# Final norm's squares summed feature-major, masks and scratch tiles prepared earlier, residual stores on ScalarE's queue

## The chip, the cores and the metric

The kernel runs on one core of a Trainium2 chip. A core has a matrix engine (TensorE, PE in the profile, with its weight loads PEld), three engines that work on 128-partition tiles (VectorE or DVE, ScalarE or ACT, GpSimd or POOL) and a fifth that only issues transfers (SyncE or SP). Every engine runs its own instruction list in order; engines wait for one another by semaphores. Transfers are put on queues by SP, ACT or POOL and moved by 16 DMA engines. The metric is device time in microseconds of one execution; less is better. Each time below is the median of several runs, or that of one profiled execution where it says so.

## What is computed

One inference step of a two-layer decoder in float32: 8 x 8 sample tokens, 16 meta tokens and a prompt of 1024, with a width of 1024.

```
def run_trunk(h, C0, n0, m0, lead, attend, prm):
    ...
            a, (C, n, m) = mlstm_mixer(rmsnorm(h, prm['norm_a'][i]), C0[i], n0[i], m0[i], lead, ...)
            h = h + a
    ...
            h = h + fox_mixer(rmsnorm(h, prm['norm_b'][j]), shared, attend,
                              prm['w_qo_b'][j], prm['q_norm_b'][j], prm['w_out_b'][j])
        h = h + swiglu(rmsnorm(h, prm['norm_ffn'][l]), prm['w_gate_up'][l], prm['w_down'][l])
        if l == N_A_LAYERS - 1:
            shared = shared_kv(h, prm['norm_kv'], prm['w_kvf'], prm['b_fg_b'], prm['k_norm_b'])
    y = rmsnorm(h, prm['norm_final'])
```

Layer A (`mlstm_mixer`) is a recurrence over chunks with 8 heads, whose gates go through a soft cap and a log-sigmoid; it returns the states C, n and m. `rmsnorm` divides by the root of the mean square over the 1024 features and multiplies by a gain. Layer B (`fox_mixer`) is attention with a per-row log-forget value over shared keys and values; the samples also attend to paged caches. `swiglu` has an inner width of 2816.

## The kernel before

Tokens are held as nine tiles (`TT`): tile 0 has the 64 sample and 16 meta tokens, tiles 1 to 8 have 128 prompt tokens each. For the FFN, the 1104 tokens are cut into four slices of 276 (`TS`). The residual H is feature-major, 8 blocks of 128 features by tokens, in SBUF as `vA` in the first layer and `Ht` in the second, and it is parked in DRAM as `hD`. A product is made of three matmuls over split operands (`mm3`, L192 to L194: high by high, low by high, high by low); a split is one ACT copy to the rounded format (L254, L266) and one DVE subtraction (L255, L267). The FFN saves products by sums of quarter blocks of the operands: `PairWeights` makes the weights' sums, `TwoNorms` those of two normed slices (`T0A`, `T0B` in the first layer, `T1A`, `T1B` in the second), the products arrive in PSUM as `m` (L1397) and `dps` (L1730).

In order of time:

- `load_x` turns the input to feature-major (`hps`, `xps`) and stores it to `hD` (L662). `phase_a` projects the values for four column groups c = 3, 0, 1, 2; with c = 3 come the gates.
- A second loop projects the query and key tiles; at its twelfth step `row_mask` (L2146 to L2151) builds two masks: POOL fills and selects, DVE reduces. The log-sigmoid of the gates (L276 to L285, result `lf_tm`) and the transposes and scans that follow (`rps` L902, scans L910 to L914, `eA`, `stk`) run beside it.
- The recurrence takes nine chunks. `chunk_scores` makes decayed scores `eb`; `f(n)` puts n steps of the output gates' projection (`mmA`) into TensorE's list as filler, out of a fixed stock, and the rest follows at the end. ACT squares the outputs for the head norm with a sum (L1256, scratch tag `jk`); the final n state goes through `nnP` and `noP`, which use the same tag. `norm_heads` and the gated heads (`ghps`, `ogeb`, `ogqk`) follow.
- The output projection adds to H (`pops`), with its weights (`wo`) split on the way in layer B; four loads of H from `hD` stand among the weight loads on SP's queue.
- In the FFN's last part (54 rounds, `seq`) each round multiplies one loaded part, `hr` from DRAM, split by ACT and DVE, with one weight part; the last rounds add to H. In the first layer `beside` puts pieces of the next norm between matmuls: root, diag (L370), spread (L377, a matmul that spreads one row over partitions into `nps`). Squares for it are summed by `add_sq` (L335 to L346). Finished slices go to `hD` (L1745, four stores on POOL's queue, on which the `hr` loads stand, too).
- `first_values` and three further groups project the shared values; after the first, c = 3, `forget` turns the log-forget values to heads on partitions (`fgps` L2082), scans them (L2087, `cnB`) and turns part of it back (`fgcq`).
- Sample attention masks queries by copying them into a zeroed tile `qmt` (L2346 memset, L2350 copies), one tile per group of four heads. Cached keys are turned by `ktp` (L2227) and copied out by `kT` (L2228). Prompt attention follows.
- `final` makes the last norm: it turns H back to tokens on partitions (`fin` L1793), squares on ACT with a sum (L1812), root, reciprocal, scales on DVE (L1818) and stores (L1823). For the tokens of tiles 6, 7 and 8 this comes after the last round.

The engines other than TensorE, and all queues, are ordered by a scheduler from estimated costs; TensorE's own order is written out by hand in the parts named here.

Of the kernel before, what the change touches and what calls it, by code (L numbers as in the profile page):

```python
# [17 lines left out]
P = 128  # L18
# [75 lines left out]
class TwoNorms:  # L94
# [30 lines left out]
    def first(self):  # L125
        self.sub(self.y1[:, self.lo], self.y2[:, self.lo], self.y1[:, self.lo])
        self.net.nc.scalar.copy(self.T[1][0], self.y1[:, self.lo])
# [12 lines left out]

    def second_c(self):
        self.low(self.x[1][:, self.lo], self.y2[:, self.lo], self.x[0][:, self.lo])
# [33 lines left out]
class Net:  # L176
# [292 lines left out]
    def mlp(self, H, raws, w, l, heads=None, cb=None):  # L469
# [5 lines left out]
        with self.pool(self.uid("nsp")) as sp, self.pool(self.uid("npp"), bufs=2, space=PSUM) as pn:  # L475
# [14 lines left out]
            with ExitStack() as c:  # L490
# [13 lines left out]
                if heads:  # L504
                    for m in range(KT):
                        for z in range(2):
                            nc.sync.dma_start(ws[m][z].bitcast(F32), self.woD[m][:, z])
                else:
                    rp = raws_open.enter_context(self.pool(self.uid("woraw"), side="right"))
                    rs = [rp.tile([P, KT, P], F32, name=self.uid("woraw")) for _ in range(6)]  # L510
                    rs = [cut(slots[0]), cut(slots[1]), *(rs[x] for x in (3, 4, 5, 2, 1, 0))]
                    for m in range(KT):
                        nc.sync.dma_start(rs[m], w[:, m * P : (m + 1) * P].rearrange("(k p) n -> p k n", p=P))
                        self.split(rs[m], *ws[m])
                        if m in (3, 5, 7):
                            for t in (0,) if m == 3 else (1,) if m == 5 else (2, 3):
                                load(nc.sync, t)
# [148 lines left out]
def phase_a(self, vt):  # L666
# [5 lines left out]
    with ExitStack() as c3:  # L672
# [14 lines left out]
        with ExitStack() as cw, self.pool("ppA0", bufs=4, space=PSUM) as pp:  # L687
            self.wpools(cw, 3, 4)
            self.load_x()
            for c in (3, 0, 1, 2):  # L690
                c0 = 2 * HA * DK + 256 * c

                def evac(i, m, ps):
                    nc.scalar.copy(v(i)[:m, 2 * c : 2 * c + 2, :DV], ps[:m, :256].rearrange("p (h d) -> p h d", h=2))
                    if c == 3:
# [3 lines left out]
                             evac)  # L699

# [31 lines left out]
        with self.pool("rowsA") as rp, self.pool("rowsAp", bufs=2, space=PSUM) as rpp, \  # L732
# [309 lines left out]
def last_state(self, C, pp, rp):  # L1042
# [5 lines left out]
    n = rp.tile([P, DV], F32, name="nnP", tag="jk")  # L1048
    nc.vector.tensor_copy(n[:, :4], C[:, :, DV])
    ps = pp.tile([P, P], F32, name="nnpP", tag="cps")  # L1050
    nc.tensor.transpose(ps[:4, :], n[:, :4], self.ident)
    no = rp.tile([P, DV], F32, name="noP", tag="jk")
# [79 lines left out]
def chunk_scores(self, i, R, rp, pp, kp, C, v, qkD, eD, wD, tm, f):  # L1132
# [12 lines left out]
    f(2)  # L1145
# [47 lines left out]
def chunk_out(self, i, R, rp, pp, kp, C, v, qkD, eD, wD, tm, den, ssq, f, sp=None, exp=None):  # L1193
# [60 lines left out]
    for h in range(HA if i else 0):  # L1254
        o = rp.tile([P, DV], F32, name=f"jk{i}{h}", tag="jk")
        nc.scalar.activation(o[:L], v(i)[:L, h, :DV], AF.Square, accum_out=ssq[:L, i, h : h + 1])  # L1256
# [92 lines left out]
def ffn(self, H, l, weights, order, TA, pn, pair, each, early, end=None):  # L1349
# [14 lines left out]
    with self.pool(f"ffn{l}") as fp, self.pool(f"ffnp{l}", space=PSUM) as pp:  # L1364
# [250 lines left out]
        with fixed(E.DVE, E.Activation):  # L1615
# [77 lines left out]
            def square(t, m):  # L1693
                if each:
                    each(t, m, count[t])
                    count[t] += 1

# [4 lines left out]
            for i, (hs, z, c) in enumerate(seq):  # L1702
# [18 lines left out]
                for m, h in [(m, h) for h in hs for m in range(4)] if apart else [(m, h) for m in range(4) for h in hs]:  # L1721
# [13 lines left out]
                    if last:  # L1735
# [3 lines left out]
                        if z in whole:  # L1739
                            t, y = whole[z]  # L1740
                            if apart:
                                square(2 * h + t - 1, 4 * y + m)
                                if m == 3:
                                    s = 2 * h + t - 1
                                    nc.gpsimd.dma_start(self.hD[:, :, TS[s][0] : TS[s][1]], H[s])  # L1745
# [34 lines left out]
def final(self, t, fp, pools):  # L1780
# [7 lines left out]
    def turn(t0, t1, ps):  # L1788
        for g in range(2):
            ps.append(pp.tile([P, 512], F32, name=self.uid("fin"), tag="d", bufs=6) if t == 3 else  # L1790
                      pn.tile([P, 512], F32, name=self.uid("fin"), tag="n"))
# [4 lines left out]
    last = [[] for _ in DONE[t]]  # L1796
    if t == 3:
        for i, ps in zip(DONE[t], last):
            turn(*TT[i], ps)
    for i, ps in zip(DONE[t], last):  # L1800
        t0, t1 = TT[i]
        L = t1 - t0
        if not ps:
            turn(t0, t1, ps)
            yield
# [18 lines left out]
        if t < 3:  # L1824
            yield
# [3 lines left out]
def first_values(self, H, pp, pn):  # L1829
# [5 lines left out]
    for tiles in ((0, 1), (5,), (2, 3), (4,), (6, 7), (8,)):  # L1835
        vs = self.ny(f"vf{tiles[0]}").rearrange("p k t -> p (k t)")[:, :512].rearrange("p (i d) -> p i d", i=2)
        for z, i in enumerate(tiles):
# [5 lines left out]
            for k in range(KT):  # L1843
                wh, wl = halves[k // 4]
# [67 lines left out]
def phase_b(self, ys, w7, cb):  # L1912
# [11 lines left out]
    with self.pool("fb", bufs=2) as fp, self.pool("fbp", bufs=2, space=PSUM) as pp:  # L1924
# [19 lines left out]
        for c in (3, 1, 2):  # L1944
# [10 lines left out]
            self.value_rows(vs, 0, cs)  # L1955
            if c == 3:
                self.forget(lf)
# [106 lines left out]
def forget(self, lf):  # L2064

    nc, I, O = self.nc, self.I, self.O
    with self.pool("fg") as fp, self.pool("fgp", bufs=1, space=PSUM) as pp:
# [7 lines left out]
        nc.gpsimd.dma_start(O["p_logf"][0, NM:].rearrange("(i p) h -> p i h", p=P), lf[:, 1:, :])  # L2075
        lt = fp.tile([HB, T], F32, name="ltB")
# [78 lines left out]
def sample_masks(self, sp):  # L2155
# [30 lines left out]
def attend_sample(self, sk, sp, s2, pp, cq, ncn, masks, Y, fill):  # L2186
# [150 lines left out]
    for g in range(2):  # L2337
# [7 lines left out]
        Q = sp.tile([P, 4, P], F32, name=f"qmt{g}", tag="qmt")  # L2345
        nc.gpsimd.memset(Q, 0.0)  # L2346
# [374 lines left out]
```

## Time and profile before

| | |
|---|---|
| median of three runs | 2867.07 us |
| lowest, highest | 2866.16, 2868.84 us |
| the profiled execution | 2865.79 us |
| its span | 2864.1 us |
| mean granted clock | 0.992 |

The span is what the profiler saw between the first and the last instruction or transfer, so the profiled execution's own time is 1.7 us longer. The row of busy times in the prediction gives, for each engine, the us in which it executed, its share and the number of instructions. A row of a timeline gives the start in us, the duration, the engine, the line, the operation, its output and inputs, shapes, a count and, in brackets, how long the engine had stood idle just before and what ended that. A row of the waits gives the total, the number and the longest of the waits of one line for one other. In the windows view a row is one stretch.

### The profile page before, as it was taken

Reading aid. Unit: us, or ns where it says so; the run is one execution under the profiler, and the core shown is the slowest. Engines: PE = TensorE matmul, PEld = TensorE weight load, DVE = VectorE, ACT = ScalarE, POOL = GpSimd, SP = SyncE. Lnnn points to the kernel's source line nnn. Section 1 sums busy time; section 2 is a strip of 40 time slices with the busy share of each in tenths; the row PEclk is TensorE's granted clock in tenths of the full one; section 3 lists DMA queues with packets and bytes.
Section 4 is the critical chain, followed back from the end, with each engine's and each line's share of the span. In section 5 each row is a group of like instructions: output and inputs, shape, how many; then the busy total and the mean of one; then the engine's idle time right before and its main releaser. Section 6 shows DMA issues by size and latency. Waiting matters only on the chain. (4 is left out here: it accounts for less than half of the span.)

```text
span 2864.1 us, 60485 instructions
## 1 busy us (share of the span) xinstructions
PE 2774.5 (97%) x23602; PEld 2660.8 (93%) x23602; DVE 1770.8 (62%) x3911; ACT 1165.3 (41%) x2288; POOL 835.1 (29%) x1295
## 2 busy tenths in 40 slices
PE   7999998999999999999999999999999999999998
PEld 7989888999999999999999888677899999999998
DVE  5142565788888655563355443677468888865656
ACT  5222363333233233443344454777433322323345
POOL 2032233223223322223363201454322232322111
PEclk9999999999999999999999999999999999999999
DMA  6365537245555365544443686443524555526556
GB/s 198 104 194 137 148 104 262 93 122 171 176 168 159 113 210 180 194 157 144 154 165 127 209 293 238 138 166 100 149 75 121 174 171 167 164 90 226 183 193 220
DMA packets 426280, 469.43 MB, mean 164 GB/s; under 512 B 41054, under 2 KB 351450, under 8 KB 424970
## 3 DMA queue, kind: packets, MB, share of 16 engines
q1 hardware_dynamic: 380066, 317.04, 35.7%
q0 software_dynamic: 44560, 147.40, 15.7%
q8 instruction: 185, 3.03, 0.4%
q10 hardware_dynamic: 1368, 1.13, 0.1%
q14 instruction: 101, 0.83, 0.1%
HBM read 318.25 MB, written 147.21 MB: 163 GB/s over the span
## 5 line engine op out<-in xcount | busy, mean ns | idle before, releaser
L1397 PE MATMUL m<-xh,slot 128*128 128x276 f32 x2752 | 540.5, 290 | 3.3 <-ACT fs L1426 3.3
L1397 PEld LDWEIGHTS m<-xh,slot 128*128 128x128 f32 x2752 | 439.7, 188 | 5.0 <-ACT fs L1426 3.7
L1397 PE MATMUL m<-xl,slot 128*128 128x276 f32 x1376 | 397.1, 289 | 0.0
L1397 PEld LDWEIGHTS m<-xl,slot 128*128 128x128 f32 x1376 | 258.7, 188 | 0.0
L192 PE MATMUL tmps<-slot,xh 128*128 128x256 f32 (+2 forms) x864 | 243.3, 282 | 0.0
L194 PE MATMUL tmps<-slot,xl 128*128 128x256 f32 (+2 forms) x864 | 240.9, 279 | 0.0
L193 PE MATMUL tmps<-slot,xh 128*128 128x256 f32 (+2 forms) x864 | 240.8, 279 | 0.0
L267 DVE TENSOR_TENSOR slot<-slot,slot 128x1024 fp32r<-128x1024 f32 x124 | 162.1, 1308 | 67.9 <-ACT slot L266 66.4
L266 ACT CAST slot<-slot 128x1024 fp32r<-128x1024 f32 x124 | 129.5, 1045 | 129.9 <-PE m L1397 111.8
L193 PEld LDWEIGHTS tmps<-slot,xh 128*128 128x128 f32 (+1 forms) x864 | 159.3, 184 | 0.1
L194 PEld LDWEIGHTS tmps<-slot,xl 128*128 128x128 f32 (+1 forms) x864 | 158.7, 184 | 0.0
L192 PEld LDWEIGHTS tmps<-slot,xh 128*128 128x128 f32 (+1 forms) x864 | 158.4, 183 | 0.1
L192 PE MATMUL mmA<-xh,whi 128*128 128x384 f32 (+1 forms) x384 | 135.0, 352 | 1.9 <-ACT stg L728 1.9
L193 PE MATMUL mmA<-xl,whi 128*128 128x384 f32 (+1 forms) x384 | 128.1, 334 | 0.0
L194 PE MATMUL mmA<-xh,wlo 128*128 128x384 f32 (+1 forms) x384 | 127.9, 333 | 0.0
L267 DVE TENSOR_TENSOR slot<-vA,slot 128x1024 fp32r<-128x1024 f32 (+1 forms) x59 | 82.2, 1396 | 32.9 <-ACT slot L266 31.7
L267 DVE TENSOR_TENSOR slot<-Ht,slot 128x1024 fp32r<-128x1024 f32 (+1 forms) x59 | 82.0, 1392 | 32.9 <-ACT slot L266 31.8
L255 DVE TENSOR_TENSOR wlo<-wraw,whi 128x1024 fp32r<-128x1024 f32 (+1 forms) x32 | 39.0, 1225 | 101.6 <-ACT whi L254 76.1
L266 ACT CAST slot<-Ht 128x1024 fp32r<-128x1024 f32 (+1 forms) x59 | 60.9, 1036 | 95.5 <-PE m L1397 88.5
L266 ACT CAST slot<-vA 128x1024 fp32r<-128x1024 f32 (+1 forms) x59 | 60.8, 1035 | 95.5 <-PE m L1397 93.5
L2543 ACT ACTIVATE s<-s,nb 128x272 f32<-128x272 f32 (+7 forms) x126 | 98.9, 786 | 0.0
L1501 DVE TENSOR_TENSOR ws<-ws 128x128 f32<-128x128 f32 x264 | 91.8, 348 | 9.0
(755 smaller groups left out, 8685.0 us busy)
## 6 DMA issues: line engine op xcount, KB each, us to landing
ws<-in_w_down SPq DMA_DIRECT2D x176, 128.0 KB
sD<-ws SPq DMA_DIRECT2D x176, 128.0 KB
slot<-sD SPq DMA_DIRECT2D x40, 512.0 KB
slot<-in_w_gate_up SPq DMA_DIRECT2D x36, 512.0 KB
kp<-in_cache_k SPq DMA_DIRECT2D x32, 512.0 KB
vp<-in_cache_v SPq DMA_DIRECT2D x32, 512.0 KB
vA<-in_w_gate_up SPq DMA_DIRECT2D x26, 512.0 KB
Ht<-in_w_gate_up SPq DMA_DIRECT2D x26, 512.0 KB
```

The lines of the kernel that those rows point to most:

```text
L192: mm(ps, sh, mh, start=first, stop=False)
L193: mm(ps, sh, ml, start=False, stop=False)
L194: mm(ps, sl, mh, start=False, stop=last)
L255: low = lambda: nc.vector.tensor_tensor(out=lo, in0=raw, in1=hi.bitcast(F32), op=ALU.subtract)
L266: self.nc.scalar.copy(hi, src)
L267: self.nc.vector.tensor_tensor(out=lo, in0=src, in1=hi.bitcast(F32), op=ALU.subtract)
L1397: nc.tensor.matmul(u.ps[h, b], w[p][:, k], x[q][:, k], start=first and k == i == 0, stop=k == 3 and i == 2, skip_group_check=True)
L1501: tt(out=o, in0=a, in1=b, op=ALU.subtract)
L2543: nc.scalar.activation(ss[z, u], ss[z, u], AF.Exp, bias=nb[:, z : z + 1], accum_out=sm[:, u, z : z + 1])
```

## The change

- The two row masks are made behind the first column group (c = 3) of `phase_a`, with tiles from another pool.
- `chunk_scores` asks for six fill steps instead of two in its first call. In the chunks 7 and 8 the squares of odd heads move from ACT to DVE; their scratch has two tags, and `nnP` and `noP` have tiles of their own.
- In `TwoNorms` three ACT copies move one job later in the list of jobs.
- In layer B's output projection the loads of H slices 0 and 1 follow the weights 4 and 6 instead of 3 and 5.
- Of the norms beside the last rounds, the spreads of slices 0 and 1 come later: at round 30 and within `first_values`. The four stores to `hD` are issued by ACT instead of POOL.
- `forget` stops after its log-sigmoid and stores, and goes on after the group c = 1.
- Both `qmt` tiles are made and zeroed in `sample_masks`.
- A class `Tail` takes the last norm of tiles 6, 7 and 8: ACT squares H feature by feature block as it becomes ready, DVE sums, three matmuls with a column of ones give the sums with tokens on partitions. The gain is applied to features 512 to 1023 before they are turned, and those twelve transposes stand ahead of the last two rounds. At the end DVE scales the lower halves and ACT the upper ones.

```
 class TwoNorms
     def first(self):
         self.sub(self.y1[:, self.lo], self.y2[:, self.lo], self.y1[:, self.lo])
-        self.net.nc.scalar.copy(self.T[1][0], self.y1[:, self.lo])
     def second_a(self):
         lo, hi, y2 = self.lo, self.hi, self.y2
+        self.net.nc.scalar.copy(self.T[1][0], self.y1[:, self.lo])
         self.sub(y2[:, lo], y2[:, hi], y2[:, lo])
-        self.net.nc.scalar.copy(self.x[0][:, lo], y2[:, lo])
     def second_b(self):
         net = self.net
+        net.nc.scalar.copy(self.x[0][:, self.lo], self.y2[:, self.lo])
         self.t2 = [net.ny(net.uid("t2")) for z in range(2)]
         for z, t in enumerate(self.t2):
             self.sub(t, self.y2[:, 4 + 2 * z : 6 + 2 * z], self.y1[:, 2 * z : 2 * z + 2])
-            net.nc.scalar.copy(self.T[2][0][:, 2 * z : 2 * z + 2], t)
     def second_c(self):
+        for z, t in enumerate(self.t2):
+            self.net.nc.scalar.copy(self.T[2][0][:, 2 * z : 2 * z + 2], t)
...
 output projection of layer B
-                        if m in (3, 5, 7):
-                            for t in (0,) if m == 3 else (1,) if m == 5 else (2, 3):
+                        if m in (4, 6, 7):
+                            for t in (0,) if m == 4 else (1,) if m == 6 else (2, 3):
...
 phase_a
+                if c == 3:
+                    for n, out in ((NQ, self.q8), (NM, self.m16)):
+                        self.row_mask(kp.tile([P, P // n, n], F32, name=self.uid("rm"), tag="rm"), out, n)
...
-                if x == 12:
-                    for n, out in ((NQ, self.q8), (NM, self.m16)):
-                        self.row_mask(rp.tile([P, P // n, n], F32, name=self.uid("rm"), tag="rm"), out, n)
...
 the n state
-    n = rp.tile([P, DV], F32, name="nnP", tag="jk")
-    nc.vector.tensor_copy(n[:, :4], C[:, :, DV])
+    n = rp.tile([P, 4], F32, name="nnP", tag="nn", bufs=1)
+    nc.vector.tensor_copy(n, C[:, :, DV])
...
 chunk_scores
-    f(2)
+    f(2 if i else 6)
...
 squares of the heads
-        o = rp.tile([P, DV], F32, name=f"jk{i}{h}", tag="jk")
-        nc.scalar.activation(o[:L], v(i)[:L, h, :DV], AF.Square, accum_out=ssq[:L, i, h : h + 1])
+        o = rp.tile([P, DV], F32, name=f"jk{i}{h}", tag=f"jk{h % 2}", bufs=1)
+        if h % 2 and i > 6:
+            nc.vector.tensor_tensor_reduce(out=o[:L], in0=v(i)[:L, h, :DV], in1=v(i)[:L, h, :DV], scale=1.0, scalar=0.0,
+                                           op0=ALU.mult, op1=ALU.add, accum_out=ssq[:L, i, h : h + 1])
+        else:
+            nc.scalar.activation(o[:L], v(i)[:L, h, :DV], AF.Square, accum_out=ssq[:L, i, h : h + 1])
...
 last rounds of the FFN
+            tail = None if each else Tail(self, fp, bank, pn, fs0[:, 1024:])
             if each:
                 for z, t in ((4, 0), (6, 1)):
                     i = 6 * z + 5
-                    beside.update({(i, 1, 1): (t, 0), (i, 2, 1): (t, 1), (i, 3, 1): (t, 2)})
+                    beside.update({(i, 1, 1): (t, 0), (i, 2, 1): (t, 1)})
+                beside[30, 0, 0] = (0, 2)
...
-                                    nc.gpsimd.dma_start(self.hD[:, :, TS[s][0] : TS[s][1]], H[s])
+                                    nc.scalar.dma_start(self.hD[:, :, TS[s][0] : TS[s][1]], H[s])
+                            elif not each and hs == (1,) and z == 6:
+                                square(3, m)
...
+                if not each and i == len(seq) - 4:
+                    tail.gains()
+                if not each and i == len(seq) - 3:
+                    tail.second()
...
-                self.first_values(H, pp, pn)
+                self.first_values(H, pp, pn, lambda: norm(1, 2))
             else:
-                for _ in end(fp, pp, 3):
-                    pass
+                tail.finish()
...
+class Tail:
+    def square(self, t, m):
+        nc, H = self.net.nc, self.net.H
+        a, b = max(TS[t][0], self.at), TS[t][1]
+        src = H[:, m, a:b]
+        o = slice(a - self.at, b - self.at)
+        c = self.count[t]
+        self.count[t] += 1
+        if c == 0:
+            nc.scalar.activation(self.sum[:, o], src, AF.Square)
+        else:
+            x = self.tmp[c % 2][:, : b - a]
+            nc.scalar.activation(x, src, AF.Square)
+            nc.vector.tensor_tensor(out=self.sum[:, o], in0=self.sum[:, o], in1=x, op=ALU.add)
+    def gains(self):
+        net = self.net
+        for k in range(4, KT):
+            x = net.H[:, k, self.at :]
+            net.nc.scalar.activation(x, x, AF.Copy, scale=net.gain[:, G_FIN + k : G_FIN + k + 1])
...
+    def second(self):
+        self.hi = [self.bank("fin"), self.bank("fin"), self.new()]
+        for x in range(3):
+            for k in range(4, KT):
+                self.turn(self.hi, x, k)
+    def finish(self):
...
+        for x in range(3):
+            nc.tensor.matmul(ps[:, x : x + 1], self.sum[:, x * P : x * P + P], net.ones[:, :1], start=True, stop=True)
+        r = fp.tile([P, 2, 3], F32, name="tr")
+        nc.scalar.activation(r[:, 0], ps[:, :3], AF.Sqrt, scale=1.0 / D, bias=net.eps)
+        nc.vector.reciprocal(r[:, 1], r[:, 0])
...
+                if g:
+                    nc.scalar.activation(o, y, AF.Copy, scale=rr)
+                else:
+                    nc.vector.scalar_tensor_tensor(out=o, in0=y, scalar=rr, in1=gr.rearrange("p (k n) -> p k n", k=4),
+                                                   op0=ALU.mult, op1=ALU.mult)
+                dst = O["y_prompt"][0, (i - 1) * P : i * P, g * 512 : g * 512 + 512]
+                nc.sync.dma_start(dst.rearrange("p (k n) -> p k n", k=4), o)
...
 first_values
+                if (i, k) == (0, 4):
+                    begin()
...
 shared values
+            if c == 1:
+                for _ in forget:
+                    pass
             if c == 3:
-                self.forget(lf)
+                forget = self.forget(lf)
+                next(forget)
...
 forget
         nc.gpsimd.dma_start(O["p_logf"][0, NM:].rearrange("(i p) h -> p i h", p=P), lf[:, 1:, :])
+        yield
         lt = fp.tile([HB, T], F32, name="ltB")
...
 sample_masks
+    self.qmt = [sp.tile([P, 4, P], F32, name=f"qmt{g}") for g in range(2)]
+    for q in self.qmt:
+        nc.gpsimd.memset(q, 0.0)
...
 attend_sample
-        Q = sp.tile([P, 4, P], F32, name=f"qmt{g}", tag="qmt")
-        nc.gpsimd.memset(Q, 0.0)
+        Q = self.qmt[g]
```

More of the change, by code (lines that the diff above doesn't have):

```diff
@@ L1047, in last_state @@
         nc.gpsimd.dma_start(O["p_C"][0, 0, a::2].rearrange("j k v -> k j v"), cs[:, :, :DV])
-    n = rp.tile([P, DV], F32, name="nnP", tag="jk")
-    nc.vector.tensor_copy(n[:, :4], C[:, :, DV])
+    n = rp.tile([P, 4], F32, name="nnP", tag="nn", bufs=1)
+    nc.vector.tensor_copy(n, C[:, :, DV])
     ps = pp.tile([P, P], F32, name="nnpP", tag="cps")
-    nc.tensor.transpose(ps[:4, :], n[:, :4], self.ident)
-    no = rp.tile([P, DV], F32, name="noP", tag="jk")
+    nc.tensor.transpose(ps[:4, :], n, self.ident)
+    no = rp.tile([P, DV], F32, name="noP", tag="no", bufs=1)
     nc.vector.tensor_copy(no[:4], ps[:4])
@@ L1696, in square @@
                     count[t] += 1
+                elif t > 1:
+                    tail.square(t, m)
             home = [((2, 0),), ((2, 2), (0, 0)), ((0, 2), (0, 4)), ((0, 6), (2, 4)), ((2, 6), (1, 0)), ((1, 2), (1, 4)),
@@ L1789, in turn @@
         for g in range(2):
-            ps.append(pp.tile([P, 512], F32, name=self.uid("fin"), tag="d", bufs=6) if t == 3 else
-                      pn.tile([P, 512], F32, name=self.uid("fin"), tag="n"))
+            ps.append(pn.tile([P, 512], F32, name=self.uid("fin"), tag="n"))
             for k in range(4):
@@ L1795, in final @@
     as_out = lambda g, a: a.rearrange("p (k n) -> p k n", k=out[g].shape[1])
[L1796 to L1800, printed above, removed]
+    for i in DONE[t]:
         t0, t1 = TT[i]
         L = t1 - t0
-        if not ps:
-            turn(t0, t1, ps)
-            yield
+        ps = []
+        turn(t0, t1, ps)
+        yield
         r = fp.tile([P, 4], F32, name=self.uid("fr"), tag="fr", bufs=3)[:L]
@@ L1823, in final, with first_values @@
                 nc.sync.dma_start(as_out(g, O["y_prompt"][0, (i - 1) * P : i * P, gs]), out[g])
-        if t < 3:
-            yield
+        yield
 @_add(Net)
-def first_values(self, H, pp, pn):
+def first_values(self, H, pp, pn, begin):
     nc = self.nc
@@ L2075, in forget @@
         nc.gpsimd.dma_start(O["p_logf"][0, NM:].rearrange("(i p) h -> p i h", p=P), lf[:, 1:, :])
+        yield
         lt = fp.tile([HB, T], F32, name="ltB")
```

26 lines of the change are left out of this document (added).

## The prediction

> **What bounds the kernel now.** I read the page's summary first, then the list of what each engine waited for, then timelines around the longest waits; fences below show rows picked from such views (start in us, us, engine, line, operation, then idle time and its releaser).
>
> ```profile
> span 2864.1 us, 60485 instructions
> PE 2774.5 (97%) x23602; PEld 2660.8 (93%) x23602; DVE 1770.8 (62%) x3911; ACT 1165.3 (41%) x2288; POOL 835.1 (29%) x1295
> PE ktp L2227 <- DVE kT L2228: 6.6, 1, 6.6
> PE nps L377 <- DVE sq L370: 6.3, 3, 4.7
> PE m L1397 <- ACT fs L1426: 3.3, 2, 1.6
> PE rps L902 <- DVE lf_tm L285: 2.9, 1, 2.9
> PE mmA L192 <- ACT stg L728: 1.9, 1, 1.9
> PE pops L194 <- DVE wo L267: 1.0, 2, 0.7
> PE fgcq L2091 <- DVE cnB L2087: 1.0, 1, 1.0
> PE fgps L2082 <- DVE lfB L285: 0.9, 1, 0.9
> ```
>
> The lower rows give total us, times and longest us. TensorE is busy for all but 89.6 us (2864.1 less 2774.5), and the change does not cut its long rounds of matmuls. So time can come only from its waits, from stretches in which its clock is low, and from the tail after its last work. The windows view shows the second; its columns are us, busy us of PE, PEld, DVE, ACT and POOL with counts, then granted clock, DMA share and GB/s.
>
> ```profile
> 165.30:172.10 6.80, 5.99 (x22) 5.22 (x23) 2.48 (x10) 1.36 (x3) 0.55 (x1) 0.50 0.55 196
> 1213.10:1216.60 3.50, 3.50 (x14) 3.25 (x15) 0.94 (x1) 2.30 (x4) 0.05 (x1) 0.51 0.38 128
> 1616.00:1622.80 6.80, 4.55 (x30) 3.98 (x30) 2.76 (x10) 0.58 (x1) 0.41 (x1) 0.50 0.78 241
> 1622.80:1630.00 7.20, 7.20 (x78) 6.34 (x72) 1.38 (x2) 1.66 (x3) 0.54 (x1) 1.00 0.98 383
> ```
>
> After three of the long waits the clock stood at half: a wait costs its own length and, behind it, half of the work done in such a stretch.
>
> **Row masks** go from the middle of the first projection to the start of the program.
>
> ```profile
> 151.77 2.35 POOL L2147 TENSOR_SCALAR_AFFINE_SELECT rm<-rm 128x8 f32<-128x8 f32 x16
> 156.45 0.42 DVE L2151 TENSOR_REDUCE rowm<-rm 128x8 f32<-128x128 f32 x1 [4.24 <-POOL rm L2149]
> 159.88 0.37 DVE L2151 TENSOR_REDUCE rowm<-rm 128x16 f32<-128x128 f32 x1 [2.50 <-POOL rm L2149]
> 166.11 2.04 PE L902 MATMUL rps<-ident,lf_tm 80*8 80x80 f32 x9 [2.87 <-DVE lf_tm L285]
> 170.21 1.23 DVE L255 TENSOR_TENSOR wlo<-wraw,whi 128x1024 fp32r<-128x1024 f32 x1 [4.25 <-DMA woD<-wlo]
> 179.78 0.44 PE L192 MATMUL mmA<-xh,whi 128*128 128x384 f32 x1 [1.88 <-ACT stg L728]
> ```
>
> DVE stood 4.24 + 2.50 us ahead of two reduces (0.42 and 0.37), all of it in the chain that ends in lf_tm, which rps needs. Without them that chain is up to 7.5 us shorter; a weight split inside it has a wait of its own, but 2.87 is all that PE needs, and the first wait goes. If the half clock goes with it, PE's work in that window, the nine transposes among it, takes 3.0 less (half of 5.99), so PE is at the second wait 5.9 sooner. What ends that second wait is a chain from rps over DVE's scans: 2.87 sooner, 1.0 more for the transposes (half of 2.04), and up to 4.25 more, because the scans stand behind the split of 170.21, whose wait for a store that POOL issues earlier now shrinks. So the chain is 3.9 to 8.1 sooner, and the restart at 179.78 no more than 5.9 + 1.88 = 7.8. I take 5.5, a little under PE's own 5.9. Low end 2.9 (the half clock stays and the second wait takes up the rest), high end 7.8. At the start POOL gains 72 operations of together about 8 us (2.35 per 16 selects, two such, the others half as many). They stand ahead of the first residual store:
>
> ```profile
> 15.11 1.03 POOL L662 DMA_DIRECT2D hD<-hs  x1 [7.98 <-ACT hs L661]
> ```
>
> That queue idled 7.98 us ahead of the store, which hides them to within some tenths; if that cover were gone, the two hs buffers come free later and the loss is about 1 us. It is inside the low end.
>
> **Query tiles.** qmt gets two tiles, zeroed much earlier; before, POOL reached the memset, behind DMA issues, at 1615.40.
>
> ```profile
> 1612.79 0.62 DVE L1993 SCALAR_TENSOR_TENSOR blo<-btp,gqk,bhi 128x384 fp32r<-128x384 f32 x1 [2.27 <-ACT bhi L1992]
> 1615.40 0.52 POOL L2346 MEMSET qmt<- 128x512 f32 x1
> 1615.95 1.52 DVE L2350 COPY qmt<-qtS 64x16 f32<-64x16 f32 x8 [2.54 <-POOL qmt L2346]
> 1617.50 0.69 DVE L2228 COPY kT<-ktp 128x512 f32<-128x512 f32 x1
> ```
>
> By the changed instruction order DVE does fifteen of the sixteen qmt copies before that blo, one after it, then kT. blo still waits for ACT, so kT ends near 1614.2 (1612.79 + 0.62 + 0.2 + 0.69, less overlap) instead of 1618.2. Gain 4.0; a wait of 2.6 remains of 6.6. The half-clock stretch behind it holds 4.55 us of work, worth 2.3. I leave it standing, since a wait of 2.87 was also followed by one (at 165.30). Ends 3.0 and 6.3.
>
> The Trainium skill, "TensorE: Matmul & The Clock Gate", section "Part 1: The HAM clock gate", says that the clock halves after at least one idle window of about 3.4 us. The trace disagrees, for the 2.87 us wait above was enough. By that page's rule the remaining 2.6 would keep full clock and this term would be 6.3; the second rival below has it.
>
> **Norms beside the last rounds, and the stores' queue.** Two spreads move behind 6 and 12 more matmuls, and four 1104 KB residual stores leave POOL's queue for ScalarE's.
>
> ```profile
> 1202.59 0.87 POOL L1745 DMA_DIRECT2D hD<-vA  x1 [3.14 <-DVE vA L1378]
> 1203.01 0.37 ACT L378 COPY sq<-nps 128x276 f32<-128x276 f32 x1
> 1206.53 0.56 POOL L1524 DMA_DIRECT2D hr<-hB_1T  x1 [3.07 <-DVE T0B_2l L267]
> 1211.42 0.42 ACT L266 CAST T0A_1h<-hr 128x276 fp32r<-128x276 f32 x1 [5.14 <-DMA hr<-hB_1T]
> 1213.09 1.17 PE L377 MATMUL nps<-sq,ones 92*128 92x276 f32 x2 [4.74 <-DVE sq L370]
> 2035.57 2.85 SPq L494 DMA_DIRECT2D Ht<-hD  x1
> hr<-hB_1T POOLq DMA_DIRECT2D x40, 276.0 KB, 4.4
> ```
>
> The two shorter nps waits are 0.8 each (6.3 less 4.74). The one in first_values I count as gained. The other is followed by the 4.74, whose end is set by a load: hr is issued at 1206.53 behind the store of 1202.59 and lands at 1211.4, in 4.9 against a median of 4.4. PE arriving 0.8 sooner only waits longer there. Off the store's queue, hr may land 0.5 earlier. So 0.8 + 0.5 = 1.3. High end 5.5: the wait vanishes wholly. Low end: each store now occupies ACT's queue. No store of this size on ACT is in the trace; nearest are POOL's issue (0.87) and SP's of the same 1104 KB (2.85, in a busy queue). Behind it on ACT stand the weight split and the hr splits, for which DVE and then PE wait. The ACT copy of 0.37 leaves that place, so a store costs 0.5 by the first price and 2.5 by the second; I take the first, because ACT's queue has nothing else in flight there. Low end −1.5.
>
> The Trainium skill, "Trainium Kernel Development and Optimization", section "Key Constraints", says that transfers issued from SP, ACT and POOL share the same 16 DMA engines and interleave, so several issuers save issue time only. By that the 0.5 would be nothing and this term 0.8; no run here shows it yet.
>
> **Smaller waits.**
>
> ```profile
> 262.09 0.64 PE L1148 MATMUL kps<-ident,qk 128*80 128x128 f32 x4 [1.45 <-DVE eb L1144]
> 447.28 0.17 DVE L1049 COPY nnP<-C 128x4 f32<-128x4 f32 x1 [1.50 <-ACT jk L1256]
> 572.47 1.12 ACT L127 CAST T0B_1h<-vA 128x1104 fp32r<-128x1104 f32 x1 [2.80 <-DVE vA L104]
> 576.49 0.38 ACT L1426 COPY fs<-m 128x276 f32<-128x276 f32 x1
> ```
>
> Four more fill steps (12 matmuls, some 1.6 us at half of the half-clock mean 5.99/22) stand ahead of kps in chunk 0 and cover its 1.45; the fill is only moved, so later chunks have four steps fewer: 1.4, ends 0 and 1.5. Odd heads' squares of the last two chunks go to DVE: nnP has its own tile but stands behind four of them there. No such square on DVE is in the trace: nnP's own four-column copy takes 0.17, a 512-wide scaling 0.7 (1.41 for two, below); nearer the first, 0.35, four make 1.4 and nnP starts where its 1.50 wait let it start; 0, ends −1.0 (a later ogeb) and 0.8. The two-norm copies one job later put ACT's fs copy, sent at 576.49 behind 1.12 us casts, about 0.6 sooner (half of one), in both layers: 1.2, ends 0 and 3.3 (the whole of that wait). The output projection's H loads one weight later: two waits of together 1.0; the weight that no longer queues behind 1104 KB lands sooner, the next one when it did, so 0.5, ends −0.5 and 1.0. The forget gates' transposes come two projections later: 0.9 vanishes; the scan's 1.0 moves with it, since as many matmuls lie between. Its scan now queues behind small DMAs on DVE and ahead of the next weight splits: 0.9, ends −1.2 and 1.9.
>
> **The tail.**
>
> ```profile
> 2852.16 2.51 PE L1793 MATMUL fin<-ident,Ht 128*128 128x128 f32 x21 [0.21 <-DVE Ht L1378]
> 2854.34 0.16 DVE L1815 RECIPROCAL fr<-fr 128x1 f32<-128x1 f32 x1 [0.36 <-ACT fr L1814]
> 2854.61 1.41 DVE L1818 SCALAR_TENSOR_TENSOR Ht<-fin,fr,sq 128x512 f32<-128x512 f32 x2
> 2855.39 5.24 SPq L1823 DMA_DIRECT2D out_y_prompt<-Ht  x6
> ```
>
> Twelve upper transposes (2.51/21 = 0.12 each, 1.4 in all) run before the last two rounds and push them back by 1.4. So the last add is done at 2853.6 instead of 2852.16. A square and a sum of 276 columns (0.4 each, as the copy of 576.49), three one-column matmuls (0.4 at most, 0.12 each), root and reciprocal (0.52, with the wait between them) bring the first scaling to about 2855.3. DVE scales three halves (0.7 each, to 2857.4) beside ACT's three, and the last issue ends near 2858.0, against 2860.6 (2855.39 + 5.24). The span ends 3.5 after that, which gives 2861.5. But six 256 KB stores now start within 2 us: 1.57 MB at the best rate above, 383 GB/s, takes 4.1, so about 2862.1. Gain 2.0, ends −0.5 (as slow as now, and part of the 1.4 lost) and 3.0.
>
> **Sum.** 5.5 + 4.0 + 1.3 + 1.4 + 0 + 1.2 + 0.5 + 0.9 + 2.0 = 16.8. The profiled execution took 2865.79, so 2849.0; the median of the runs is 2867.07, 1.3 more, so 2850.3, or **2850**.
>
> **Rivals.** (1) *The waits only move*: each freed chain meets the next one. What remains is 2.9 (rps) + 4.0 (qmt) + 0.8 (spread) + 1.4 (fill) = 9.1, less 1.4 for the transposes ahead of an unchanged tail: 7.7, so 2859. For it: 1.88 follows 2.87 and 4.74 follows 0.8. Against it: rps, kT and mmA hang on chains which themselves start sooner. (2) *The clock stays full* behind the shortened qmt and spread waits: 2.3 + 1.7 (half of 3.50) more, so 2846. For it: the waits are shorter. Against it: 2.87 sufficed. (3) *Slower: the stores block ScalarE.* If each issue holds ACT for longer than SP's 2.85, say 4.5, squares and splits behind it are late; four cost 18 and the 1.3 is lost, so 2850 + 19 = 2869. It decides from about 4 us an issue (16.8 to be lost). Against it: 0.87 on POOL, an empty queue on ACT. (4) *The squares on DVE and the copies do not do what they say*: those terms are 0 and 0, so 2851; this lies inside the forecast.
>
> **How the numbers follow.** Forecast (2847.5 to 2855, rival 4 within it) 0.52; the waits move 0.28; clock stays full 0.13; stores block 0.07. The range 2845 to 2862 takes in the forecast, the second rival and most of the first, which its own unknown terms spread over 2855 to 2863. A measurement here can tell 0.2%, 5.7 us: "faster" is below 2861.3, "slower" above 2872.8. Of the first rival three quarters lie below 2861.3; of the last, half above 2872.8: faster 0.86, same 0.10, slower 0.04.
>
> **What would show it.** Right: no rps wait, and full clock where 165 to 172 was; ktp wait near 2.6; no kps, fgps or first nps wait; the two-norm fs wait about 1.0; stores on ACT under 1 us; last output issue about 2.5 us sooner than now. Wrong: an mmA wait of 4 or more after rps, ACT store issues of some us with splits late behind them, or output stores that drain for more than 5 us after the last issue.

## The result, and the profile after

The changed kernel takes 2871.7 us (median of 20 runs, 2867.72 to 2880.28) against 2866.39 (20 runs, 2862.45 to 2869.17): a ratio of 1.0023, with an interval of 1.0016 to 1.0031. So it is slower by 5 us, where 17 less were forecast. Its profiled execution took 2877.98 us and is one of its slower ones: its span is 12.2 us longer than that of the kernel before, where the medians differ by 5.3.

The page's head and the list of waits of TensorE in that execution (total us, times, longest) read:

```profile
span 2876.3 us, 60505 instructions
PE 2778.6 (97%) x23608; PEld 2663.7 (93%) x23608; DVE 1779.4 (62%) x3933; ACT 1166.3 (41%) x2279; POOL 833.7 (29%) x1291
```

```profile
PE sp L2605 <- DMA kh<-kDh: 7.2, 1, 7.2
...
PE fgcq L2178 <- DVE cnB L2174: 6.7, 1, 6.7
...
PE nps L378 <- DVE sq L371: 5.4, 1, 5.4
PE nps L1232 <- issue: 4.9, 1, 4.9
...
PE nnpP L1052 <- DVE nnP L1050: 3.1, 1, 3.1
PE ktp L2317 <- DVE kT L2318: 2.9, 2, 2.6
...
PE m L1402 <- ACT fs L1431: 1.8, 2, 0.9
```

Most of what was to go is gone or smaller: no rps wait on lf_tm, no fgps wait on lfB, ktp 2.6 instead of 6.6. But two waits are now near the top: a new one of 7.2 us (sp), and fgcq, which had 1.0 before and now has 6.7. The first one has a low clock behind it. Windows after the masks and at the first scores of prompt attention (us, busy us by engine, granted clock, DMA share, GB/s):

```profile
165.00:172.00 7.00, 7.00 (x44) 6.96 (x45) 7.00 (x13) 1.99 (x4) 1.59 (x3) 1.00 0.34 103
...
1783.00:1795.00 12.00, 8.02 (x29) 6.63 (x30) 2.25 (x16) 2.19 (x5) 4.32 (x10) 0.50 0.95 351
```

Totals do not tell where time came from and where it went. For that the same matmul is looked up in both traces. The table gives by how many us matmuls start later than before (negative: sooner), at times of the kernel before; each number is the median over those within 2 us. Columns are the changed kernel and two of the experiments below: one early query tile (E3), and that with the forget gates as before (E5).

| time before | what lies ahead of it | changed | E3 | E5 |
|---|---|---|---|---|
| 150 | start, values | 0.8 | 2.5 | 1.2 |
| 258 | masks, gates' chain | −6.1 | −4.7 | −4.6 |
| 448 | recurrence | −2.5 | −7.8 | −6.8 |
| 1190 | most of the first FFN | −1.9 | −8.1 | −7.0 |
| 1340 | norms beside, stores, first values | −2.5 | −9.1 | −8.0 |
| 1370 | forget gates | 3.9 | −2.9 | −8.4 |
| 1620 | query tiles | −0.6 | −7.4 | −12.8 |
| 1774 | sample attention | 0.2 | −6.1 | −11.4 |
| 1781 | first scores of prompt attention | 15.1 | −4.6 | −10.0 |
| 2060 | prompt attention, output projection | 11.6 | −7.3 | −15.1 |
| 2800 | second FFN | 11.5 | −5.9 | −15.3 |
| end | tail | 12.2 | −5.2 | −14.5 |

The changed kernel loses 6.4 us at the forget gates (−2.5 to 3.9) and 14.9 at the start of prompt attention (0.2 to 15.1). Everything else together gains, although 3.6 us are also lost within the recurrence (−6.1 to −2.5), where E3 and E5 gain 3.1 and 2.2; that is the nps L1232 wait of 4.9, which the last section takes up.

### The profile page after: what moved, and what is told of

Its sections match the earlier page's. It is cut to its first block, busy times and chain, and to the rows that moved or that the text cites. A ratio compares the mean times of both kernels' runs of the same rounds, so it can differ in the third digit from the quotient of the medians.

```text
span 2876.3 us, 60505 instructions
## 1 busy us (share of the span) xinstructions
PE 2778.6 (97%) x23608; PEld 2663.7 (93%) x23608; DVE 1779.4 (62%) x3933; ACT 1166.3 (41%) x2279; POOL 833.7 (29%) x1291
## 3 DMA queue, kind: packets, MB, share of 16 engines
q0 software_dynamic: 43472, 142.88, 15.1%
```

## Experiments

The medians below are each from 5 to 12 runs, beside the kernel before on the same chip; that one gave 2867.18, 2866.81, 2865.29 and 2868.48 in the four sets. The interval of a ratio is some 0.0013 to either side with five runs, which is 3.7 us. So two experiments that lie less than that apart are told apart by their traces, not by their medians; where this is done by matmuls looked up in both traces, the numbers are those of the table's kind, on the time scale of the kernel before.

**The first scores (E1, E2, E3).** SP's queue before and after shows what is late. It issues the loads of prompt attention; kernel before, then the changed one:

```profile
1762.67 0.42 SPq L2435 DMA_DIRECT2D qh<-qDh  x1
```

```profile
1762.52 0.33 SPq L2426 DMA_DIRECT2D vmS<-vD  x1
1778.66 0.34 SPq L2524 DMA_DIRECT2D qh<-qDh  x1
```

The same queue, at the same place in its order, sends qh 16 us later. Just ahead of that, POOL issues the last store of an output gate:

```profile
1776.33 0.58 POOL L2140 DMA_DIRECT2D og2D<-ogb  x1 [1.60 <-ACT ogb L2139]
```

That store lands at 1778.5, and SP's list of waits names it:

```profile
SPq L2524 <- DMA og2D<-ogb: 15.5, 1, 15.5
```

By the semaphores in the two traces, the qh load of the changed kernel waits for ACT and for transfers of POOL's queues, that of the kernel before for one transfer on SP's own. Nothing in the diff touches qh. But two early qmt tiles, in a pool that opens sooner, replace one slot in a later pool, so that 2 KB a partition more are held and the pools behind move up. The first qh tile would then lie where the gate output tiles (ogb) were; the traces hold no addresses, so this is inferred from what the load waits for.

E1 takes the two tiles back:

```
-    self.qmt = [sp.tile([P, 4, P], F32, name=f"qmt{g}") for g in range(2)]
-    for q in self.qmt:
-        nc.gpsimd.memset(q, 0.0)
...
-        Q = self.qmt[g]
+        Q = sp.tile([P, 4, P], F32, name=f"qmt{g}", tag="qmt")
+        nc.gpsimd.memset(Q, 0.0)
```

> The changed kernel with only the query tiles put back: one qmt tile in the sample attention's pool, zeroed where it was. Theory: the two early qmt tiles shift the pools behind them by 2 KB a partition, so that prompt attention's first qh tile lies on memory of the gate output tiles (ogb), and its load on SP has to wait for their stores; undone, SP sends qh near 1763 again, the sp waits of 7.2 + 1.2 + 0.8 + 1.2 us and the low clock behind them go (about 14 us of delay between 1775 and 1780), and the ktp wait is 6.6 again (3.7 lost): 2861 us. Rival (the loads are late because of the other parts, such as the forget gates' later transfers): the sp waits stay and the time is 2875.

Measured: 2862.58 us. No sp wait for a transfer is left in its list, and ktp waits 6.2 again.

E2 adds the two tiles alone to the kernel before.

> The kernel before with only the two early qmt tiles added. Theory of shifted memory: 3.7 us are won at ktp and 14 lost at the first sp, 2876 us, with qh sent by SP near 1779. Rival: the early tiles only bring the 4 us, 2862.

Measured: 2876.9 us, ratio 1.0043 (1.0030 to 1.0056). The one edit makes the new wait and brings the small gain, as its waits show:

```profile
SPq L2437 <- DMA og2D<-ogb: 15.7, 1, 15.7
...
PE sp L2518 <- DMA kh<-kDh: 7.3, 1, 7.3
...
PE ktp L2230 <- DVE kT L2231: 3.5, 2, 2.7
```

E3 keeps the tile early, but takes only one, zeroed again for the second group:

```
-    self.qmt = [sp.tile([P, 4, P], F32, name=f"qmt{g}") for g in range(2)]
-    for q in self.qmt:
-        nc.gpsimd.memset(q, 0.0)
+    self.qmt = sp.tile([P, 4, P], F32, name="qmt")
+    nc.gpsimd.memset(self.qmt, 0.0)
...
-        Q = self.qmt[g]
+        Q = self.qmt
+        if g:
+            nc.gpsimd.memset(Q, 0.0)
```

> The changed kernel with one qmt tile, made and zeroed early as in the change, and zeroed again for the second group, so that the pools' total is as before. Theory of shifted memory: ktp wait stays near 2.6, the sp waits go, 2858 us. Rival (being early itself is what delays the loads): 2872.

Measured: 2856.88 us, ratio 0.9964 (0.9951 to 0.9977). SP sends qh right behind vmS again, and ktp's wait on DVE is 2.1 at the longest:

```profile
1756.21 0.33 SPq L2425 DMA_DIRECT2D vmS<-vD  x1
1756.58 0.42 SPq L2525 DMA_DIRECT2D qh<-qDh  x1
```

So neither the early zeroing nor another part of the change is the cause: it is the second early tile, and with it the memory that it takes. Of all runs, only the three with two early tiles (the changed kernel, E2, E4) have SP waiting on og2D<-ogb, 15.5 to 15.7 us each.

**The forget gates (E4, E5, E8).** The timeline, kernel before (DVE) and then the changed one (DVE, POOL and TensorE):

```profile
1348.61 2.31 DVE L2087 TENSOR_TENSOR_SCAN cnB<-onB,ltB 16x1040 f32<-16x1040 f32 x1 [3.15 <-ACT ltB L2083]
...
1369.32 0.70 DVE L2136 TENSOR_TENSOR ncn<-cnew,rowm 128x8 f32<-128x8 f32 x8 [4.11 <-DMA cnew<-csN]
```

```profile
1361.62 0.91 POOL L2219 DMA_DIRECT2D cnew<-csN  x1 [2.59 <-DMA csN<-cscn]
1364.55 0.70 DVE L2223 TENSOR_TENSOR ncn<-cnew,rowm 128x8 f32<-128x8 f32 x8 [6.22 <-DMA cnew<-csN]
1365.18 2.31 DVE L2174 TENSOR_TENSOR_SCAN cnB<-onB,ltB 16x1040 f32<-16x1040 f32 x1
1367.54 1.03 PE L2178 MATMUL fgcq<-ident,cnB 16*128 16x16 f32 x8 [6.68 <-DVE cnB L2174]
```

The scan's input was ready 5.6 us before the scan began (ltB ends at 1359.55), but eight small additions stand ahead of it in DVE's order and wait for `cnew`, the last of a chain of three small transfers. DVE sat idle for 6.22 us with the scan behind them, and TensorE for 6.68. E4 puts the gates back:

```
-            if c == 1:
-                for _ in forget:
-                    pass
             if c == 3:
-                forget = self.forget(lf)
-                next(forget)
+                self.forget(lf)
...
-        yield
```

> The changed kernel with the forget gates done at once after the group c = 3, as before. Theory: the scan on DVE no longer stands behind eight small operations that wait for a chain of three small transfers; the fgcq wait of 6.7 becomes 1.0 and the fgps wait of 0.9 is back: 4.7 us and some low clock less, 2866. Rival (the freed time is taken up by the late qh load, whose end other work sets): 2871.

Measured: 2865.64 us, 6 below the changed kernel; in its list fgcq waits 1.1 and fgps 0.9. E5 is E3 with this edit:

> The changed kernel with one early qmt tile and with the forget gates done at once after c = 3. Theory: the two terms that failed are independent, so the gain over the kernel with one early tile (2856.9) is again some 6.9 us, what was lost between 1340 and 1370: 2850. Rival (the freed time is taken up by the waits behind): 2854.

Measured: 2850.8 us, ratio 0.9944 (0.9931 to 0.9957). The two losses are independent and add up. E8 instead keeps the split of E3 and resumes after c = 2 (`if c == 2:` in place of `if c == 1:`):

> The changed kernel with one early qmt tile, and the second half of the forget gates a further projection later, after c = 2, when the eight small DVE operations and their transfers are long done. Theory (DVE's order is the cause, not the splitting): the fgcq wait is 1 us or less and the fgps wait stays away, 2850, or 1 less than with the gates done at once. Rival (the splitting itself costs, by a scan ahead of the next weights): a new wait of several us at the next projection, 2856.

Measured: 2851.83 us, with this one wait left:

```profile
PE fgcq L2178 <- DVE cnB L2174: 1.1, 1, 1.1
```

Splitting the gates costs nothing; where their second half stands in DVE's order does.

**The masks alone (E7)**, in the kernel before:

> The kernel before with only the row masks moved to the start. Theory: 7 us less by the time of the first chunk (rps without a wait, full clock behind it, mmA sooner), kept to the end: 2860. Rivals: 5.5 as I forecast, 2861.5; the second wait takes up the rest, 2.9, 2864; the masks delay the first residual stores, 2866.

Measured: 2860.47 us, ratio 0.9974 (0.9964 to 0.9984): 6.3 less. The rps wait on lf_tm is gone and the clock behind it full:

```profile
165.00:172.00 7.00, 6.73 (x43) 6.24 (x42) 5.09 (x11) 1.64 (x4) 1.16 (x2) 1.00 0.73 224
```

**The tail (E6, E9, E13 to E15).** The last adds of H in the changed kernel, with Tail's sums between them, and the six output stores:

```profile
2860.74 0.44 DVE L1383 TENSOR_TENSOR Ht<-Ht,dps 128x276 f32<-128x276 f32 x1 [2.69 <-PE dps L1739]
2861.68 0.45 DVE L1815 TENSOR_TENSOR fs<-fs,nr 128x276 f32<-128x276 f32 x1 [0.50 <-ACT nr L1814]
2862.05 0.43 DVE L1383 TENSOR_TENSOR Ht<-Ht,dps 128x276 f32<-128x276 f32 x1
...
2868.34 4.13 SPq L1863 DMA_DIRECT2D out_y_prompt<-Ht  x6
```

Each sum waits for ACT's square of the block just added, and the next add waits behind it: the adds are 1.3 us apart. The stores take 4.13 us to issue, 0.69 each on average. E6 is E5 with the old last norm: no `Tail`, all transposes, squares and scales after the last round.

> The same, and the last norm as before (no Tail, all 24 transposes and the squares after the last round). Theory: the sums on DVE between the last adds hold TensorE back by 0.5 us a time and the six output stores queue behind one another, so that the tail cost 0.7 instead of gaining 2.0: 2849, that is 0.7 less than with Tail, and adds again 0.76 apart. Rival (my forecast of the tail): 2852.

Measured: 2849.22 us, ratio 0.9941 (0.9928 to 0.9953), 1.6 less than E5. E9 is E5 with Tail's sums on POOL (`nc.gpsimd.tensor_tensor` in `square`):

> The changed kernel with one early qmt tile, the forget gates at once, and in Tail the sums of squares on POOL instead of DVE. Theory (DVE's sum, which waits for ACT's square, stands between two adds of H and holds TensorE): the last four adds are 0.76 apart again instead of 1.32, the three fin waits of 0.4 to 0.8 shrink, a sum on POOL takes 0.4 longer at the end: 2849.5, 1.3 under the same kernel with the sums on DVE. Rival (the six output stores, issued close together, set the end anyhow): 2851.

Measured: 2852.3 us. The adds are back to 0.76 us apart, and though POOL takes 0.79 for a sum, the last sum ends 4.74 us after the start of the first of the four adds (2835.57 to 2840.31), where E5 takes 5.41 (2834.03 to 2839.44). The median, 1.5 above E5's, does not show these 0.7 us. Three more experiments separate the sums from the stores; E13 issues the stores of the upper halves from POOL:

```
-                nc.sync.dma_start(dst.rearrange("p (k n) -> p k n", k=4), o)
+                (nc.gpsimd if g else nc.sync).dma_start(dst.rearrange("p (k n) -> p k n", k=4), o)
```

> The changed kernel with one early qmt tile and the forget gates at once (2850.8), the three stores of Tail's upper halves issued by POOL instead of SP. If the one queue sets the end, the last issue on SP is 1.5 to 2 sooner and so is the end: 2849. If the transfers themselves set it (1.57 MB at once), the end stays: 2850.8.

Measured: 2850.16 us. All six are issued within 2.5 us, but from the first issue to the end of the span it takes 8.7 us (2844.82 to 2853.5), where the one queue took 7.9 (2868.34 to 2876.3); E15 below, with two queues, takes 8.7 too:

```profile
2844.82 1.69 SPq L1863 DMA_DIRECT2D out_y_prompt<-Ht  x3
```

E14 keeps each sum back until the next add stands ahead of it (a list `late` in Tail, emptied at the next `square` and in `finish`):

> The same kernel (2850.8) with each of Tail's sums on DVE put behind the next block's add instead of ahead of it, stores on SP as in the change. If DVE's sums hold TensorE, the last four adds are about 0.85 apart instead of 1.32, the two fin waits on them of 0.4 to 0.6 go, and the end is 1.2 sooner: 2849.6. If not, 2850.8.

Measured: 2849.2 us. DVE's order is now add, sum of the block before, add, with no wait between:

```profile
2835.75 0.44 DVE L1383 TENSOR_TENSOR Ht<-Ht,dps 128x276 f32<-128x276 f32 x1 [2.27 <-PE dps L1739]
2836.11 0.44 DVE L1818 TENSOR_TENSOR fs<-fs,tq 128x276 f32<-128x276 f32 x1
2836.50 0.44 DVE L1383 TENSOR_TENSOR Ht<-Ht,dps 128x276 f32<-128x276 f32 x1
```

E15 does both:

> Both edits. If both causes hold and add up: 2847.9, faster than with the last norm as before (2849.2). If the transfers set the end, whatever is done ahead of them moves it only by the time at which the first starts: 2849.6.

Measured: 2849.5 us, not the 2847.9 of two causes that add up. The medians of this group lie too close together to decide (E13 to E15 stand beside 2868.48 for the kernel before, E5 and E6 beside 2866.81). The traces decide: the waits between the adds are gone with the sums out of the way. From the matmuls at 2845 to the end of the span, measured against the kernel before, E5 loses 2.2 us, E14 1.3, E13 3.2 and E15 2.2, while E6 with the old norm gains 0.2. So the sums between the adds cost 0.9, the second queue costs 0.9 to 1.0 instead of gaining, and without either of them Tail is still 1.5 behind the old norm. Issued sooner, the stores do not land sooner.

**Smaller parts, each taken out of E6 (2849.2).** E10 has the residual stores on POOL's queue (`nc.gpsimd.dma_start`):

> The fastest kernel so far (one early qmt tile, forget gates at once, last norm as before: 2849.2), with the four residual stores on POOL's queue again. Theory: all queues share the transfer engines, hr lands 0.2 later at the most; the nps wait is 5.5 instead of 5.4 and the time 2849.4. My forecast: 0.5 later, 2849.7. Rival (POOL's issue of 0.87 delays the hr loads by that and more): 2851.

Measured: 2851.24 us, within the medians' error of E6, and the wait grows from 5.3 in E6 to 6.0:

```profile
PE nps L378 <- DVE sq L371: 6.0, 1, 6.0
```

The half clock behind it ends 3.1 us after the wait, in E6 4.8 us after it, and this gives the 0.7 back: from 1190 to 1340 E10 gains 0.5 us on the kernel before, E6 0.6.

E11 has `f(2)` in the first chunk:

> The same fastest kernel with two fill steps instead of six in the first chunk. Theory: the kps wait of 1.45 is back, and the fill that it covers is spent elsewhere: 1.4 more, 2850.6. Rival (the six steps only move the wait to the loads of qq, which the first chunk waits for next): 2849.2, with a kps wait of 1.4 and a smaller one at nps L1232.

Measured: 2848.25 us, no loss in the median, as the rival had it. The waits of E11 and then E6:

```profile
PE kps L1149 <- DVE eb L1145: 2.5, 3, 1.4
...
PE nps L1232 <- issue: 0.6, 1, 0.6
```

```profile
PE nps L1232 <- issue: 1.5, 1, 1.5
PE kps L1149 <- DVE eb L1145: 0.8, 1, 0.8
```

With six steps kps waits 1.7 less in all, but nps L1232, which needs a chain of transfers (qwD, qq) that begins after kps, waits 0.9 more: about half only moves. By the matmuls looked up, E6 gains 1.0 us from 258 to 560, E11 loses 0.3. E12 has the copies of TwoNorms where they were:

> The same fastest kernel with the two-norm copies of TwoNorms where they were. Theory: the m wait for ACT's fs copy is 1.6 again instead of 0.9 in both layers, the wait for T0B_4l takes back 0.2 of it: 0.5 a layer, 1.0 in all, 2850.2. Rival (DVE sets the pace there and takes it all back): 2849.2.

Measured: 2848.63 us, no loss in the median, though the wait is 3.3 in two again, against 1.8 in E6:

```profile
PE m L1401 <- ACT fs L1430: 3.3, 2, 1.6
```

A median of five can't show the 1 us in question, but the matmuls looked up can: across the two stretches with these copies, 560 to 580 and 2140 to 2790, E6 gains 0.7 and 0.6 on the kernel before, E12 0.0 and −0.1. So the theory holds, and not the rival.

The measured times of E6, E11, E12, E14 and E15 (2848.3 to 2849.5) can't be told apart. All beat the kernel before by some 0.6%.

## Why the prediction was wrong

**Query tiles: the step that failed.** The prediction put "Gain 4.0; a wait of 2.6 remains of 6.6", and that came out to the tenth in this execution (2.0 to 2.7 in the other traces with early tiles). The half clock that it left standing behind the wait was 3.4 us long instead of 6.8, or absent. What the prediction left out is that a tile made early is also memory held early. It costed the edit on the engines alone; the 14.9 us came from memory: a load that nothing in the diff touches now waits for the store of another buffer, which by all signs it overwrites. E2 shows the whole, 9.7 us lost by this edit alone. That the load waits for these stores is shown by SP's waits in the three runs with two early tiles, and that the second tile is the reason by E3, which keeps the earliness and gives back the memory.

**Forget gates: the term that was mis-sized.** The prediction named the mechanism, "Its scan now queues behind small DMAs on DVE", and gave it a low end of −1.2. It was worth −6.4 net (0.9 and 1.0 saved, 6.7 lost, and some low clock). The lateness of the small transfers could have been read from the trace before: the eight additions landed there long after the scan, and the changed order put them ahead of it.

**The tail: mis-sized, a loss.** Forecast 2.0 gained; by the medians the kernel without it is 1.6 faster (E6 against E5), which is within their error, and by the traces Tail loses 2.1 us in the changed kernel from 2845 to the end, and 2.2 in E5. Two steps failed. The sums between the adds were counted at the end only, not as 1.3 instead of 0.76 us from each of the last four adds to the next. And the stores were let drain at "383 GB/s, takes 4.1" us: by the prediction's own times (first issue near 2856.0, end 2862.1) they need some 6 us from the first issue to the end; it took 7.9, with all issued within 4.1. Between the first issue and the end of the old tail lie 8.7 us (2855.39 to 2864.1), with the issues spread over 5.2: little can be gained there by issuing sooner.

**Masks: right.** 5.5 forecast, 6.3 measured alone. The rps wait and the half clock went: from 150 to 258 the changed kernel gains 6.9 us, E7 5.8. The start may have paid for it. All fifteen traces with early masks reach 150 later than the kernel before, by 0.7 to 4.7 us (the table's first row has three of them, E7 3.9), while E2, without them, is 2.0 sooner. The prediction allowed about 1 us for this, as part of its low end; how much of it the masks cause was not tested.

**Fill and copies: right steps, too small for the medians.** 1.4 and 1.2 were forecast, and the medians of E11 and E12 show nothing. The traces show more. The copies gain 0.7 to 0.8 us from 560 to 580 in all thirteen traces that have the edit, 0.4 to 0.6 of it kept until 1190, and 0.2 to 0.6 in the second layer: together about the 1.0 that E12 was expected to lose. The rest moves to other waits, mainly nps L360 on ACT's squares (1.2 in E12, 1.9 in E6). With six fill steps, ten of thirteen traces gain 0.3 to 2.9 us from 258 to 560, while E2, E7 and E11, with two, lose 0.1 to 0.3. The three others lose 2.9 to 4.6 there by the long wait at nps L1232. So the first rival, that waits only move, holds for a part of the fill and little of the copies. **The squares on DVE** were put at 0; the nnpP wait went from 3.5 to 3.1.

**Norms and stores: about right.** The two 0.8 us spreads became one wait of 5.4 (4.74 plus what TensorE came sooner); 1.3 forecast, 0.6 measured in the table (1.0 in E3 and E5). The stores' queue alone is worth 0.7 at that wait (E10), but 0.1 in what is left of it at 1340, where 0.5 was forecast. The issue on ACT costs 0.5 to 0.6 each, the nearer of the two prices. From its own issue to its landing, the first hr load behind the second store takes 4.6 to 4.7 us in the thirteen traces with the stores on ACT's queue, 4.9 in the kernel before, E2 and E7, and 5.6 in E10, all four with the stores on its own queue. The Trainium skill, "Trainium Kernel Development and Optimization", section "Key Constraints", lets several issuers save issue time only; these 0.2 to 1.0 us are more than that.

**The H loads** brought about 1.4 (13.0 at 2030 to 11.6 at 2060 in the changed kernel) where 0.5 was forecast. No run has this edit taken out of the changed kernel; E2 and E7, which lack it, gain 0.2 over the same stretch. In five traces (E3, E6, E8, E9, E10) 1.8 to 2.2 us are lost again by 2120.

The slower rival, stores that block ACT, did not come about. E6, in which the three failed terms are taken back or mended, takes 2849.2, beside a forecast of 2850 for all of it; that the sum fits so well is partly chance, since the tail's 2.0 are missing from it and the masks and the H loads gained more than their terms.

## What to carry to other kernels

A tile that is made earlier can move the pools behind it. Before costing such an edit at nothing, compare, in the compiled programs, what the loads of the following stage wait for. An operation that is moved stands behind everything that is in its engine's order there; ask when the last of those is released, not how long they run. A small sum that waits for another engine must not stand between two operations for which TensorE waits.

## What was not expected of the hardware

- In the changed kernel's profiled execution nps L1232 waited 4.85 us, 4.0 in E8's and 4.2 in E13's, against 0.9 to 1.5 in the other ten traces with six fill steps and 0.5 to 0.6 in the four with two. In the changed kernel's, the third of the four loads of qq landed 5.7 us after its issue (262.91 to 268.56); in E6's it took 2.6. A half clock from 266.5 to 273.3 went with the wait. The cause was not found; whether the six fill steps make this wait possible was not tested.
- The length of a wait alone does not tell whether a half clock follows. The ktp waits of the fourteen traces with early tiles are 2.0 to 2.7 us long. In ten of them the granted clock was 0.50 for 3.4 us near the end of the wait or just behind it, for example with 2.6 in the changed kernel (mean 0.79 from 1616 to 1624) and 2.0 in E6. In four it stayed full, with 2.7 (E2), 2.2 (E8), 2.1 (E3) and 2.0 (E14).
- Six output stores of 256 KB need 7.9 to 8.7 us from the first issue to the end, whether issued by one queue or two and within 2.5 or 5.2 us.
